# Memory attention at the start of layer 1, pair steps dealt out by table, six state updates moved into the output projection, and an own PSUM bank for the first query and the first forget gate

## The chip, the cores and the metric

The kernel is one launch on one core of a Trainium2 chip. The metric is device time in microseconds (us): 906.13 us is the median of three runs of the kernel before (906.07 to 907.13). Engines are named as in the profile: PE is the matrix engine (PEld its weight loads), DVE, ACT and POOL are the vector, scalar and general engines, SP issues most loads. L303 is line 303 of the kernel whose profile is read; lines of the changed kernel are a few higher.

## The reference, cut to what matters

One inference step of a decoder with two layers, for 256 prompt tokens and 8 sample tokens (264 columns) of width 2048. Layer 0 mixes tokens by windowed attention, layer 1 by a gated recurrence (HGRN2) with 12 heads, whose state is 128x128 for each head and sample. In both, 4 more heads attend to a memory of 256 rows, a SiLU gate multiplies all 2048 channels, and one output projection, a residual and a LayerNorm follow.

```python
def _hgrn2_chunked(q, k, v, logf, s0):
...
    state = jnp.exp(g_last)[..., None] * state + jnp.einsum('bshk,bshv->bhkv', k_dec, vc)
...
def _hgrn_branch(h, w_in, lb, norm_w, s0):
    q, f, iv, mq, g = _split(jnp.einsum('btd,de->bte', h, w_in), HG_SPLITS)
    fg = lb[None, None, :] + (1.0 - lb[None, None, :]) * jax.nn.sigmoid(f.astype(jnp.float32))
    qh = jax.nn.silu(q.astype(jnp.float32)).reshape(b, t, HG_HEADS, HG_DK)
    kh = (1.0 - fg).reshape(b, t, HG_HEADS, HG_DK)
...
    o, s_new = _hgrn2_chunked(qh, kh, vh, gh, s0.astype(jnp.float32))
    o = o * lax.rsqrt(jnp.mean(jnp.square(o), axis=-1, keepdims=True) + RMS_EPS) \
        * norm_w.astype(jnp.float32).reshape(HG_HEADS, HG_DV)
...
def _mem_attend(mq, mk, mv):
    s = jnp.einsum('bthd,bmhd->bhtm', mq, mk).astype(jnp.float32) * (MEM_HD ** -0.5)
    p = jax.nn.softmax(s, axis=-1)
    return jnp.einsum('bhtm,bmhd->bthd', p.astype(mv.dtype), mv)
```

## The kernel before, in words

**The stream of units.** The kernel is a stream of 172 units, most of them a block of 128x2048 fp32 (1 MB): a weight's 2048 input rows by 128 output columns, a block of a memory cache, or a state. SP loads a unit into one of four `raw` buffers (L76 to L82). `prep` (L84) splits it into a high and a low fp16 half in one of four `hl` buffers: ACT writes the high half (L97), DVE the low half (L98). Four `hl` buffers mean that unit n+4 is split only when PE has done with unit n. A weight unit is then 48 matmuls of 128x264 (three for each of 16 blocks, L303, L304, L305), accumulated in one PSUM bank. The eight last units of the output projection are split into buffers of their own (`held`).

**PSUM.** Eight banks with fixed tags: two `pj` for projections, two `pt` for small transposes and products, two `sc` for scores, one `pv`, one `ms`. A tag with two buffers is handed out in turn, in program order: whoever asks third waits for the first to be read.

**Layer 1 before.** For each of six pairs of heads come the units f, f, v, v, q, state, q, state: forget gates (`f_unit`), values (`hv_unit`), queries (`hq_unit`) and the two heads' states in half units of 512 KB (`state_unit`). For heads 0 to 7 a gate unit stands behind each state. Then come four memory query units (mq), eight memory cache units (ck, cv) between gate units 8 to 15, and 16 units of the output projection (o). `hv_unit` reads its bank at L1034 (`hvt`) and L249/L251 (`vs`, the sample tokens' values); one unit later `hv_rows` transposes them on PE (`hvp`, L1045, and `hvr`, L1048) and copies them out. The tile `vs` is one buffer for each head parity: it can't be written before `hvr` of the pair before has read it, and the `pj` bank is free only when `vs` is written.

**The side chain of a pair.** `hg_side` (L1064) computes the prompt part of the recurrence for two heads. It is a generator; after each unit, `pump(1)` issues one step of it. Its steps are hd, seven levels hs, pk, pu, hpo (L1117 to L1171), and rms (L1182), with `osb` (L1173), `osq` (L1177), a Ln and an Exp on ACT (L1183, L1186, each with a table load), and the scaled result on DVE (L1189). It takes `sc`, `pt` and `pv` banks between the units' own uses.

**State update before.** Inside each `state_unit`, after its eight products for the sample outputs (`hos`), eight matmuls with a selection matrix spread the values (`vb`, L1233), ACT scales the state by the forget gate (L1237, 8 instructions per head), DVE adds key times value (L1238, 8 per head), and POOL stores the new state (`out_ss`, L1241).

**What sets the order.** Every engine works through its own list in order, and that list is fixed when the kernel is built: a scheduler takes the program's order as priority and places each instruction where, by its own durations, it is ready. What waits in a list holds up all that is behind it in that list.

## Time and profile before

| | before |
|---|---|
| median of three runs | 906.13 us |
| profiled execution: time, span, mean clock | 906.08 us, 904.3 us, 0.994 |
| PE busy | 886.6 us (98%) |
| DVE, ACT busy | 701.5 us (78%), 582.4 us (64%) |
| bytes moved | 198.67 MB, 220 GB/s |

The span goes from the first instruction to the last; the execution's own time is 1.8 us longer. PE's busy time counts from a matmul's start to its modelled end, so that matmuls which follow each other without a gap overlap in it; a gap appears as "idle before", with the instruction that ended the wait. PEclk is the clock that PE was granted, as a share of full speed.

### The profile page before, as it was taken

To read this page: it belongs to the slowest core of one execution; us is meant where nothing else is said; L and a number is where in the kernel's file an instruction comes from. 1 tells how busy PE (TensorE), PEld (TensorE's weight loads), DVE (VectorE), ACT (ScalarE), POOL (GpSimd) and SP (SyncE) were. 2 spreads that over 40 slices of the span, in tenths; PEclk is the share of its full clock that TensorE was granted. 3 is DMA by queue.
4 is the path that set the end of the run, shared out by engine and by line. 5 is a ranking of instruction groups with operands and counts; after the bars stand their busy time and mean duration, and the time that the engine had idled before them with its cause. 6 is when DMAs were issued, how large, how long until landed. Compare 5 with 4: busy or idle time off the path is not lost.

```text
span 904.3 us, 21814 instructions
## 1 busy us (share of the span) xinstructions
PE 886.6 (98%) x9281; PEld 762.9 (84%) x9281; DVE 701.5 (78%) x1230; ACT 582.4 (64%) x982; POOL 34.9 (4%) x68
## 2 busy tenths in 40 slices
PE   9999999999999999999999999999999999799996
PEld 6888889678888888876888888898888888688996
DVE  6879877669886666697687887979788989678736
ACT  6767776657664444476766877777777585858415
POOL 1100010000000000002000000000000000000000
PEclk9999999999999999999999999999999999899999
DMA  9998566557785555556374655827454878456303
GB/s 340 392 353 317 188 245 209 188 208 265 262 333 192 187 192 203 207 198 214 127 292 137 216 201 174 299 101 260 160 215 164 303 283 308 172 207 244 130 2 97
DMA packets 37853, 198.67 MB, mean 220 GB/s; under 512 B 4555, under 2 KB 10732, under 8 KB 17532
## 3 DMA queue, kind: packets, MB, share of 16 engines
q1 hardware_dynamic: 33024, 181.55, 56.3%
q0 software_dynamic: 4688, 15.67, 4.6%
q8 instruction: 72, 1.18, 0.5%
q14 instruction: 25, 0.20, 0.1%
q10 hardware_dynamic: 44, 0.07, 0.0%
HBM read 180.03 MB, written 17.22 MB: 218 GB/s over the span
## 4 chain that ended last, share of the span: by engine, by line
PE 77%; DVE 8%; ACT 6%; DMA 6%; issue 3%; SPq 0%; ACTq 0%; DVEq 0%
PE o L303 5%; PE o L305 5%; PE o L304 5%; PE g L305 5%; PE g L303 5%; PE g L304 5%; DVE hl L98 4%; ACT hl L97 2%; PE hv L305 2%; PE hv L303 2%; PE hv L304 2%; DMA raw<-in_w_in 2%; PE hq L303 2%; PE hq L305 2%; PE hq L304 2%
## 5 line engine op out<-in xcount | busy, mean ns | idle before, releaser
L98 DVE SCALAR_TENSOR_TENSOR hl<-raw,hl 128x2048 f16<-128x2048 f32 (+2 forms) x168 | 358.6, 2138 | 82.0 <-ACT hl L97 81.0
L97 ACT ACTIVATE hl<-raw 128x2048 f16<-128x2048 f32 (+2 forms) x168 | 299.2, 1784 | 97.8 <-PE o L305 45.4
L305 PEld LDWEIGHTS <-hl 128*128 128x128 f16 (+2 forms) x2048 | 197.4, 98 | 31.8 <-DVE hl L98 2.9
L303 PEld LDWEIGHTS <-hl 128*128 128x128 f16 (+2 forms) x2048 | 197.3, 98 | 30.6 <-issue 2.2
L304 PEld LDWEIGHTS <-hl 128*128 128x128 f16 (+2 forms) x2048 | 197.4, 98 | 30.3 <-issue 2.2
L305 PE MATMUL g<-xhl,hl 128*128 128x264 f16 x512 | 142.0, 277 | 2.4 <-DVE hl L98 2.4
L303 PE MATMUL g<-xhl,hl 128*128 128x264 f16 x512 | 141.9, 277 | 0.0
L304 PE MATMUL g<-xhl,hl 128*128 128x264 f16 x512 | 141.9, 277 | 0.0
L303 PE MATMUL o<-mix,hl 128*128 128x264 f16 x384 | 105.4, 276 | 0.8 <-DVE xres L747 0.8
L304 PE MATMUL o<-mix,hl 128*128 128x264 f16 x384 | 105.8, 276 | 0.0
L305 PE MATMUL o<-mix,hl 128*128 128x264 f16 x384 | 105.7, 276 | 0.0
L303 PE MATMUL q<-xhl,hl 128*128 128x264 f16 x192 | 53.0, 276 | 1.0 <-DVE kst L251 1.0
L303 PE MATMUL f<-xhl,hl 128*128 128x264 f16 x192 | 52.9, 276 | 0.4 <-DVE mvhl L251 0.4
L305 PE MATMUL hv<-xhl,hl 128*128 128x264 f16 x192 | 53.0, 276 | 0.0
L303 PE MATMUL hq<-xhl,hl 128*128 128x264 f16 x192 | 53.0, 276 | 0.0
L304 PE MATMUL hq<-xhl,hl 128*128 128x264 f16 x192 | 53.0, 276 | 0.0
L305 PE MATMUL hq<-xhl,hl 128*128 128x264 f16 x192 | 53.0, 276 | 0.0
L304 PE MATMUL hv<-xhl,hl 128*128 128x264 f16 x192 | 53.0, 276 | 0.0
L303 PE MATMUL hv<-xhl,hl 128*128 128x264 f16 x192 | 53.0, 276 | 0.0
L304 PE MATMUL q<-xhl,hl 128*128 128x264 f16 x192 | 53.0, 276 | 0.0
L305 PE MATMUL q<-xhl,hl 128*128 128x264 f16 x192 | 53.0, 276 | 0.0
L304 PE MATMUL f<-xhl,hl 128*128 128x264 f16 x192 | 52.9, 276 | 0.0
(338 smaller groups left out, 1858.4 us busy)
## 6 DMA issues: line engine op xcount, KB each, us to landing
raw<-in_w_in SPq DMA_DIRECT2D x88, 1024.0 KB, 6.4
raw<-in_w_o SPq DMA_DIRECT2D x32, 1024.0 KB, 5.0
raw<-in_w_mk SPq DMA_DIRECT2D x8, 1024.0 KB, 4.9
raw<-in_w_mv SPq DMA_DIRECT2D x8, 1024.0 KB, 4.9
raw<-in_c_mk SPq DMA_DIRECT2D x8, 1024.0 KB, 5.1
raw<-in_c_mv SPq DMA_DIRECT2D x8, 1024.0 KB, 7.0
raw<-in_state SPq DMA_DIRECT2D x12, 512.0 KB, 5.4
out_ss<-raw POOLq DMA_DIRECT2D x12, 512.0 KB, 5.5
```

Source lines behind the costliest of these rows:

```text
L97: hi = self.nc.scalar.activation(hl[:, 0, s], raw[:, s], AF.Copy, scale=scale)
L98: lo = self.nc.vector.scalar_tensor_tensor(hl[:, 1, s], raw[:, s], scale, hl[:, 0, s], op0=ALU.mult, op1=ALU.subtract)
L303: mm(out, lhs(0), rhs(0), start=start, stop=False)
L304: mm(out, lhs(0), rhs(1), start=False, stop=False)
L305: return mm(out, lhs(1), rhs(0), start=False, stop=stop)
```

## The change

The changed kernel computes the same; one scale moves from the keys into the selection matrix. It does this:

- **Own bank, high halves first.** q0 (the first projection of layer 0's queries) and f0 (the first unit of layer 1) accumulate in the `pv` bank instead of a `pj` bank, with all 32 products of the weight's high half first and the 16 of its low half last.
- **Memory attention first.** Layer 1 begins with f0, the four mq units and then the eight cache units, dealt between f1, v0, v1, q0, two gates, q1, f2 and f3. The four memory side chains (`memp_side`) run there too.
- **Pair steps by table.** `pump` takes the number of steps from a table: 0 after cache and state units, 2 after most f and v units, 1 otherwise. Before it was 1 after every unit.
- **States by pair.** One unit holds the states of two heads (1 MB). Heads 0 to 5 are updated there, one head at once and one a unit later; the `raw` buffer is held one unit longer.
- **Six updates put off.** For heads 6 to 11 the state unit only copies the forget gates and keys behind the spread values (`vr`) and stores that to DRAM (`kept`, 80 KB for a pair). POOL loads it back into `late_kept`, and loads each state a second time into the memory attention's old tiles `mkhl`, `mvhl`, `mqhl` ("homes"). The update runs as `late_update`, attached to output units 1, 3, 5, 7, 9 and 11; the loads of heads 9, 10 and 11 need a home whose store has landed.
- **Gates.** Only heads 0, 1, 2 and 6 have their gate early; all others, those of heads 10 and 11 last, stand between the pairs and the output units.

Three places show what the scheduler makes of it. In names the number behind the word is the head or the pair (hvr6: head 6; hpo2: pair 2 of heads 4 and 5), behind the underscore stands a buffer.

First, PE in layer 1 around the values and queries of heads 6 to 9. Before:

```order
L303 MATMUL hv7_8148<-xhl_93,hl113_7897 128x264
...
L303 MATMUL hq6_8231<-xhl_93,hl114_7992 128x264
...
L1152 MATMUL pk2_8214<-ident_66,qk32_4_7165 128x128 x4
L1045 MATMUL hvp6_8221<-ident_66,hvt6_8110 128x128 x2
...
L1048 MATMUL hvr6_8225<-ident16_68,vs0_5659 128x128
L1158 MATMUL pu2_8283<-vn4_7321,kn2_8219 128x128 x4
```

After:

```order
L1166 MATMUL pu2_8658<-vn4_7926,kn2_8599 128x128 x4
L1053 MATMUL hvp6_8681<-ident_66,hvt6_8545 128x128 x2
...
L309 MATMUL hv9_9267<-xhl_96,hl127_8979 128x264
L1179 MATMUL hpo2_8669<-qk32_4_7736,s12_8663 128x128
...
L1056 MATMUL hvr6_8685<-ident16_68,vs0_5662 128x128
L1053 MATMUL hvp7_8755<-ident_66,hvt6_8545 128x128 x2
...
L1056 MATMUL hvr7_8759<-ident16_68,vs1_5663 128x128
...
L307 MATMUL hq8_9343<-xhl_96,hl128_9076 128x264
```

The transposes of head 6's values (hvp6, hvr6), which stood inside the query unit of the same head, now stand one pair of heads later, at and behind the end of hv9, and directly ahead of the query unit of head 8.

Second, ACT at the same two places, where the values are read from their bank. Before (heads 6 and 7):

```order
L1034 ACTIVATE hvt6_8110<-hv6_8059 128x264
L249 ACTIVATE vs0_5659<-hv6_8059 128x8
L97 ACTIVATE hl116_8145<-raw116_7840 128x2048
L1079 ACTIVATE qk16_1_5654<-qk32_4_7165 128x2x8x32
L1079 ACTIVATE qk16_2_5655<-qk32_4_7165 128x2x4x64
L1034 ACTIVATE hvt6_8110<-hv7_8148 128x264
L249 ACTIVATE vs1_5660<-hv7_8148 128x8
```

After (heads 8 and 9; hl127 is hv9's unit, so that hl131 takes its buffer):

```order
L100 ACTIVATE hl131_9338<-raw131_8982 128x2048
L1181 ACTIVATE osb2_8187<-hpo2_8669 128x2x256
L1009 ACTIVATE qk32_8_9034<-th8_9036,hl_lb_88 128x256
L1009 ACTIVATE qk32_8_9034<-th9_9130,hl_lb_88 128x256
L1054 ACTIVATE vn6_8543<-hvp7_8755 128x256
L1042 ACTIVATE hvt8_9226<-hv8_9175 128x264
L253 ACTIVATE vs0_5662<-hv8_9175 128x8
L1042 ACTIVATE hvt8_9226<-hv9_9267 128x264
L253 ACTIVATE vs1_5663<-hv9_9267 128x8
L1185 ACTIVATE osq20_8677<-osb2_8187 128x264
L1185 ACTIVATE osq21_8679<-osb2_8187 128x264
L1213 ACTIVATE mkhl_100<-mkhl_100,late_kept_10622 128x128 x5
```

The readers of head 8's value bank (hvt8, vs0) now stand behind a split of a whole unit and the tail of pair 2, and a put-off state's scaling follows at once.

Third, DVE where pair 5 ends and its two mixes are made for the output projection. Before:

```order
L1164 SCALAR_TENSOR_TENSOR s25_10571<-s15_10570,prod5_10089,pu5_10565 128x128 x2
L671 TENSOR_SCALAR mrnm1_10691<-mrnm1_10691 32x1
L673 RECIPROCAL mrz1_10692<-mrz1_10692 32x1
L674 TENSOR_SCALAR mrows1_10690<-mrows1_10690,mrz1_10692 32x256
L251 SCALAR_TENSOR_TENSOR msphl1_10701<-mback1_10698,msphl1_10701 128x64
L1189 SCALAR_TENSOR_TENSOR mix_95<-osb5_9734,small_t_64,osq50_10644 128x264
```

After:

```order
L1172 SCALAR_TENSOR_TENSOR s25_10690<-s15_10689,prod5_10066,pu5_10684 128x128 x2
L1214 SCALAR_TENSOR_TENSOR mkhl_100<-vb60_11142,late_kept_10622,mkhl_100 128x128 x4
L1214 SCALAR_TENSOR_TENSOR mkhl_100<-vb61_11155,late_kept_10622,mkhl_100 128x128 x4
...
L1214 SCALAR_TENSOR_TENSOR mqhl_99<-vb80_11438,late_kept_10622,mqhl_99 128x128 x4
L1197 SCALAR_TENSOR_TENSOR mix_98<-osb5_10087,small_t_64,osq50_10763 128x264
L1197 SCALAR_TENSOR_TENSOR mix_98<-osb5_10087,small_t_64,osq51_10765 128x264
L1214 SCALAR_TENSOR_TENSOR mqhl_99<-vb81_11451,late_kept_10622,mqhl_99 128x128 x4
L737 SCALAR_TENSOR_TENSOR sil110_10951<-sil110_10951,mix_98 128x264
L737 SCALAR_TENSOR_TENSOR sil111_11011<-sil111_11011,mix_98 128x264
L739 TENSOR_TENSOR mix_98<-sil110_10951,mix_98 128x264
```

Where the memory softmax of the sample tokens stood, there are now 24 additions of the put-off updates of heads 6, 7 and 8 (three tiles, eight each), and the two mixes of pair 5 stand among them. Before, PE met this end of pair 5 inside gate unit 13; after, it meets it inside output units 10 and 11, whose last matmuls read these mixes.

The diff, cut to what the prediction speaks of:

```diff
-NG1 = 8
+EARLY = (0, 1, 2, 6)
+LATER = tuple(range(6, HD))
...
-            while free < prepped and (free <= i or self.units[free][5]):
+            while free < prepped and (free + self.longer.get(free, 0) <= i or self.units[free][5]):
...
-    def proj(hl, src, n, name, cols=slice(None), tag="pj"):
+    def proj(hl, src, n, name, cols=slice(None), tag="pj", apart=False):
         w = hl.rearrange("p s (c f) -> p s c f", c=NC)
+        if apart:
+            pt = bank("pv", 1, name)
+            for k, (c, s, r) in enumerate([(c, 0, r) for c in range(NC) for r in range(2)] + [(c, 1, 0) for c in range(NC)]):
+                mm(pt[:, :n], w[:, s, c], src[:, r, c, cols], start=k == 0, stop=k == 3 * NC - 1)
+            return pt[:, :n]
...
-            pt = proj(hl, xhl, T, f"f{h}")
+            pt = proj(hl, xhl, T, f"f{h}", apart=h == 0)
...
-                cur["vr"] = p1.tile([P, 2, P], F16, tag="vr", name=f"vr{h}", bufs=2)
+                cur["vr"] = p1.tile([P, 2, KEPT], F32, tag="vr", name=f"vr{h}", bufs=2)
...
+    def update(h, R, vr, fgs, ks, sel):
+        for g in range(2):
+            pvb = bank("pt", 2, f"vb{h}{g}")
+            for bb in range(4):
+                mm(pvb[:, bb * P : (bb + 1) * P], sel[:, 4 * g + bb], vr, start=True, stop=True)
+            for bb in range(4):
+                b = 4 * g + bb
+                s = R[:, b]
+                nc.scalar.activation(s, s, AF.Copy, scale=fgs[:, b : b + 1])
+                nc.vector.scalar_tensor_tensor(
+                    s, pvb[:, bb * P : (bb + 1) * P], ks[:, b : b + 1], s, op0=ALU.mult, op1=ALU.add
+                )
+        nc.gpsimd.dma_start(ss_o[h // 2, :, h % 2 * TS * P : (h % 2 + 1) * TS * P], R.rearrange("p b v -> p (b v)"))
+
+    homes = deque()
+    aside = {}
+
+    def fetch(h):
+        if not homes:
+            aside["sel"] = cp.tile([P, TS, P], F16, tag="ms", name="late_sel", bufs=2)
+            nc.gpsimd.dma_start(aside["sel"], sel_d)
+            aside["kept"] = cp.tile([P, len(LATER), KEPT], F32, tag="ms", name="late_kept", bufs=2)
+            for pi in sorted(kept):
+                k = 2 * pi - LATER[0]
+                nc.gpsimd.dma_start(aside["kept"][:, k : k + 2], kept[pi])
+            for t in (mkhl, mvhl, mqhl):
+                names = "abcd"[: len(t.shape) - 1]
+                homes.append(t.bitcast(F32).rearrange(f"p {' '.join(names)} -> p ({' '.join(names)})")[:, : TS * P])
+        homes.rotate(-1)
+        aside[h] = homes[-1]
+        nc.gpsimd.dma_start(aside[h], state[h // 2][:, (h % 2) * TS * P : (h % 2 + 1) * TS * P])
+
+    def late_update(h):
+        k = aside["kept"][:, h - LATER[0]]
+        R = aside[h].rearrange("p (b v) -> p b v", b=TS)
+        update(h, R, k[:, : P // 2].bitcast(F16), k[:, P // 2 : P // 2 + TS], k[:, P // 2 + TS :], aside["sel"])
+
+    def with_update(fn, k):
+        def f(hl):
+            fn(hl)
+            late_update(LATER[k])
+            if k + 3 < len(LATER):
+                fetch(LATER[k + 3])
+
+        return f
+
...
+            if 2 * pi in LATER:
+                tail = vr[:, :, P // 2 :]
+                nc.vector.tensor_copy(tail[:, :, :TS], fgs)
+                nc.vector.tensor_copy(tail[:, :, TS:], ks)
+                nc.gpsimd.dma_start(kept[pi], vr)
+                return
+            R = raw.rearrange("p (i b v) -> p i b v", i=2, b=TS)
+
+            def half(i):
+                update(2 * pi + i, R[:, i], vr[:, i, : P // 2].bitcast(F16), fgs[:, i], ks[:, i], H["sel"])
+
+            half(0)
+            later.append(lambda: half(1))
 
         return fn
 
...
+    state_at, pumps = {}, {}
+
+    def w1(part, i, fn, n=1):
+        pumps[len(stream.units)] = n
+        stream.add(wb(w_in1, NB1[part] + i), fn)
+
+    def state_of(pi):
+        at = state_at[pi] = len(stream.units)
+        pumps[at] = 0
+        whole = 2 * pi not in LATER
+        if whole:
+            stream.longer[at] = 1
+        stream.add(state[pi], state_unit(pi), SA, whole=whole)
+
...
+    f_of(0)
+    for h in range(NM):
+        w1("mq", h, mem1_sides(mq_unit(h)) if h == NM - 1 else mq_unit(h))
+    cache(c_mk, ck_unit, 0)
+    f_of(1, 2)
+    cache(c_mk, ck_unit, 1)
+    v_of(0, 2)
+    cache(c_mk, ck_unit, 2)
+    v_of(1)
+    cache(c_mk, ck_unit, 3)
+    q_of(0)
+    gate_of(0)
+    cache(c_mv, cv_unit, 0)
+    gate_of(1)
+    cache(c_mv, cv_unit, 1)
+    q_of(1)
+    cache(c_mv, cv_unit, 2)
+    f_of(2, 2)
+    cache(c_mv, cv_unit, 3)
+    f_of(3, 2)
+    state_of(0)
+    v_of(2, 2)
+    v_of(3, 2)
+    q_of(2)
+    q_of(3)
+    state_of(1)
+    gate_of(2)
+    for pi in range(2, HD // 2):
+        gated = 2 * pi - 2 in EARLY
+        f_of(2 * pi, 2)
+        f_of(2 * pi + 1, 2)
+        v_of(2 * pi, 2)
+        v_of(2 * pi + 1, 1 if gated else 2)
+        q_of(2 * pi)
+        q_of(2 * pi + 1)
+        state_of(pi)
+        if 2 * pi in EARLY:
+            gate_of(2 * pi)
...
+    for k, j in enumerate([j for j in range(NC) if j not in EARLY and j not in last] + list(last)):
+        w1("g", j, fetch_first(gate_unit(1, j)) if k == 6 else gate_unit(1, j))
     for i in range(NC):
-        stream.add(wb(w_o[1], i), out_unit(1, i), home=hold if i >= NC - NSPLIT else None)
+        unit = out_unit(1, i)
+        if i % 2 == 1 and i // 2 < len(LATER):
+            unit = with_update(unit, i // 2)
...
-        pump(1)
+        pump(pumps.get(i, 1))
...
```

## The prediction

> **What bounds the kernel now.** I read the page, then the windows of stages, the waits of PE, and the timeline of PE in the stretch with the waits. The page first:

> ```profile
> span 904.3 us, 21814 instructions
> PE 886.6 (98%) x9281; PEld 762.9 (84%) x9281; DVE 701.5 (78%) x1230; ACT 582.4 (64%) x982; POOL 34.9 (4%) x68
> ```

> PE bounds it. An edit counts only where it changes PE's work or PE's idle time. Windows of layer 1 (span, PE, PEld, DVE, ACT, POOL busy; then granted clock, DMA share, GB/s):

> ```profile
> 420.00:762.00 342.00, 341.60 (x3685) 302.55 (x3685) 285.65 (x530) 246.93 (x419) 14.69 (x27) 1.00 0.61 216
> 762.00:790.00 28.00, 22.50 (x280) 18.23 (x278) 20.70 (x31) 21.19 (x32) 0.54 (x1) 0.88 0.54 195
> ```

> In 342 us of pair work PE stands still for 0.4 us. In the next 28 us, where pair 5's end, the memory softmax and the last gates meet, it stands still for 5.5 us at a clock of 0.88. PE's waits inside 762 to 790, then two of the whole run:

> ```profile
> PE g L305 <- DVE hl L98: 2.4, 2, 1.7
> PE hpo L1169 <- ACT st L1147: 1.5, 1, 1.5
> PE mback L677 <- DVE mrows L674: 1.0, 1, 1.0
> PE msc L303 <- ACT osq L1183: 0.4, 1, 0.4
> PE hpo L1171 <- ACT s L1162: 0.3, 1, 0.3
> ```

> ```profile
> PE q L303 <- DVE kst L251: 1.0, 1, 1.0
> PE f L303 <- DVE mvhl L251: 0.4, 1, 0.4
> ```

> The timeline around the longest of these gaps (start, us), and the windows of two throttled stretches (columns as above):

> ```profile
> 783.32 0.27 PE L303 MATMUL g<-xhl,hl 128*128 128x264 f16 x1
> 783.43 0.27 PE L304 MATMUL g<-xhl,hl 128*128 128x264 f16 x1
> 785.43 0.40 PE L305 MATMUL g<-xhl,hl 128*128 128x264 f16 x1 [1.73 <-DVE hl L98]
> 785.63 0.43 PE L303 MATMUL g<-xhl,hl 128*128 128x264 f16 x1
> 785.85 0.43 PE L304 MATMUL g<-xhl,hl 128*128 128x264 f16 x1
> ```

> ```profile
> 777.00:781.00 4.00, 3.63 (x54) 2.85 (x53) 0.67 (x2) 3.96 (x7) 0.00 (x0) 0.64 0.27 107
> 785.40:788.10 2.70, 2.67 (x13) 1.84 (x14) 2.70 (x5) 2.70 (x6) 0.00 (x0) 0.50 0.50 161
> ```

> A weight's matmul starts 0.11 us after the one before (48 make 5.4 us for a unit); after the gap of 1.73 us they start 0.22 us apart for 2.7 us. So this stretch loses 5.5 us of idle time, 1.4 us (0.36 of 4.0) and 1.35 us (half of 2.7) by the clock, and 0.17 us in each of its six gaps, since a gap is counted from the modelled end (0.28 after the start) where the next matmul could have come 0.11 after it: 9.3 us in all.

> **The change, part by part.** *Own bank, high halves first.* q0 waits for the bank that kst is read from, f0 for that of mvhl, the one 1.0 and the other 0.4 us, with 0.17 each: 1.7 us. In the `pv` bank both waits go; the low halves come 32 matmuls (3.6 us) later than before, so nothing is late next. −1.7 us.

> *Memory attention first.* The softmax and the cache units leave the stretch 762 to 790 and stand beside the first pairs, where no side chain of a pair is behind yet. I count the whole −9.3 us there, and judge what comes back by the ends of the pairs, next.

> *The pairs.* Two steps a unit put pk and pu ahead of hvp in the turn of the two `pt` banks, and pair p's chain now ends while pair p+1's values are projected (first place of the change). The query unit that follows needs the `pj` bank that `vs` is read from; `vs` needs `hvr` of the pair before, and ACT's readers stand behind a unit's split and the chain's tail. The durations, from ACT's timeline in 600 to 640, 545 to 600, and 762 to 790:

> ```profile
> 607.87 0.58 ACT L1173 ACTIVATE osb<-hpo 128x512 f32<-128x512 f32 x1
> 608.35 1.90 ACT L97 ACTIVATE hl<-raw 128x2048 f16<-128x2048 f32 x1
> 610.15 0.73 ACT L1177 ACTIVATE osq<-osb 128x264 f32<-128x264 f32 x2
> 613.74 1.28 ACT L1183 ACT_TABLE_LOAD   x1
> 615.04 0.85 ACT L1183 ACTIVATE osq<-rms,eps_rms 128x264 f32<-128x264 f32 x2
> 634.55 0.59 ACT L1001 ACTIVATE qk<-th,hl_lb 128x256 f32<-128x256 f32 x1
> ```

> ```profile
> 587.04 2.44 ACT L1237 ACTIVATE raw<-raw,fg 128x128 f32<-128x128 f32 x8
> 589.89 0.38 ACT L1034 ACTIVATE hvt<-hv 128x264 f32<-128x264 f32 x1
> 590.16 0.17 ACT L249 ACTIVATE vs<-hv 128x8 f16<-128x8 f32 x1
> ```

> ```profile
> 771.06 0.36 ACT L1147 ACTIVATE st<-hs 64x256 f32<-64x256 f32 x1
> 771.32 0.58 ACT L1154 ACTIVATE kn<-pk 128x512 f32<-128x512 f32 x1
> 773.15 0.38 ACT L1162 ACTIVATE s<-pu 128x256 f32<-128x256 f32 x1 [1.25 <-PE pu L1158]
> ```

> From one start to the next a split takes 1.80, osb 0.48, hvt 0.27: each 0.1 less than its row. On PE and DVE:

> ```profile
> 772.02 1.09 PE L1158 MATMUL pu<-vn,kn 128*128 128x128 f32 x8
> 774.13 0.39 PE L1170 MATMUL hpo<-st,vn 128*128 128x128 f32 x2
> 774.35 0.39 PE L1171 MATMUL hpo<-qk,s 128*128 128x128 f32 x2
> 776.01 1.16 PE L1182 MATMUL rms<-osq,ones_rms 128*128 128x264 f32 x4
> ```

> ```profile
> 567.61 1.90 DVE L1238 SCALAR_TENSOR_TENSOR raw<-vb,ks,raw 128x128 f32<-128x128 f32 x7
> 570.43 2.29 DVE L98 SCALAR_TENSOR_TENSOR hl<-raw,hl 128x2048 f16<-128x2048 f32 x1
> ```

> All times below count from the end of the pair's second value unit; 0.2 us is my estimate for a hand-over between engines.

> - *hq6 (A).* The same list as in the second place of the change, for head 6, and here both rms stand ahead of hq6. ACT: split 1.80, osb 0.48, two qk 0.98, vn and hvt 0.54, vs 0.06, hvt and vs 0.33, osq 0.4, so 4.6, and 4.8 on PE. Then two rms (1.0) and a vb: hq6 starts at 6.0. PE has 2.8 us of its own there (four hpo at 0.22, two rms, some 0.9 of small ones). Stall 3.2.
> - *hq8 (B).* Up to vs 4.0, on DVE behind the split's low half (1.9 + 2.2): hq8 starts at 4.5, with 1.2 of PE's own. Stall 3.3.
> - *hq10 (C).* Here PE has even pk, hpo and pu behind hv11. Split 1.8, st and kn 0.85, pu 0.93, s 0.4, four hpo 0.9, osb, qk, vn, hvt, vs 2.2, and hand-overs 0.6: hq10 starts at 7.7, with 3.5 of PE's own. Stall 4.2.

> *The put-off updates beside them.* For pairs 3 and 4, ACT's scalings of `mkhl` and `mqhl` stand ahead of the Ln that frees the `sc` bank for hd3 and hd4. They wait for `late_kept`: a store and a load in turn on POOL's queue, 80 KB each. Such transfers aren't in the trace; the nearest rows are

> ```profile
> ident<-in_ident POOLq DMA_DIRECT2D x1, 64.0 KB, 3.8
> out_sp<-s POOLq DMA_DIRECT2D x6, 128.0 KB, 3.1
> raw<-in_state SPq DMA_DIRECT2D x12, 512.0 KB, 5.4
> out_ss<-raw POOLq DMA_DIRECT2D x12, 512.0 KB, 5.5
> ```

> I take 3.8, the nearest in size, with 3.1 and 5.5 as ends. B: the values are copied at 2.3, loaded back at 9.9; five scalings at 0.30, a table load 1.3 and a Ln 0.5 make 13.2; PE comes to hd3 at 11.3 (hq8, two rms, part of hq9). Stall 1.9 (0.5 to 5.3). C: copied at 6.3, back at 13.9, eight scalings, table, Ln: 18.1; PE is there at 14.1. Stall 4.0 (2.6 to 7.4). [...]

> *Output units 10 and 11 (D).* Times from the end of pu5. DVE's adds take 0.26 each. The first can start at 2.4, when PE has done the 19 matmuls of o11 ahead of vb60; five groups of four are done at 7.85. ACT's chain from hpo at 3.3 (osb, osq, rms, table, two Ln 0.85, table, Exp) brings the mixes' factors at 8.6; the two mixes take 0.9 (264 columns each, an estimate from osq's row, as for Exp and the gate products), four more adds 1.0, two gate products and ACT's product after them 1.0: o10 goes on at 11.5. PE's own: 2.1, hpo 0.9, rms 1.0, eight groups vb 1.8, so 5.8. Stall 5.7. Then vb101 and o12 need head 9's state, whose load waits for head 6's store in the same tile: issued at 4.7, 5.5 and 5.4 later it is there at 15.7; eight scalings, one add and one residual add end at 18.9. PE comes there at 15.9 (36 matmuls). Stall 3.0. D is 8.7.

> *Work that changes without weight.* The second read of six states (3 MB), the kept tiles and the larger state loads go beside DMA engines that are busy 61% in the pairs; twelve ones products less save PE 0.3 us at most; DVE saves some small splits while it isn't the bound. Nothing, as long as weights arrive a unit ahead; if that cover went, a late unit would cost up to its 5.4 us.

> *Clock.* A gap of 1.73 us cost 1.35 more; the gaps of 1.0 (q0) and 0.4 (f0) cost none that I see. Six of the stalls are 1.9 us or longer; D's first is in pieces. Between 0 and 6 x 1.35 = 8.1, I take 4.0, the middle. [...]

> **The sum**, against the profiled execution's 906.1 (span 904.3 and 1.8 around it; the median of the runs is 906.13, the same): −1.7 −9.3 +3.2 +(3.3+1.9) +(4.2+4.0) +8.7 +4.0 = +18.3, so 924.4.

> **The rivals.** *Nothing comes in place (faster).* If the readers of the value banks were through ACT's list, and the kept tiles back, before PE asks at hq6, hq8, hq10 and o10, only −11.0 would be left: 895. For it: 342 us of the same work with 0.4 us idle, ACT at 64%. Against it: PE's list shows the small steps of a pair's end in one heap ahead of hq6, hq8 and hq10, where nothing else is left to cover them, as it was at 769 to 778. It decides where ACT's lists run 3 to 4 us shorter than added up here.

> *Only the lists, not the loads.* If DMAs land early enough and the clock holds, A, B, C and the first of D stay: 3.2 + 3.3 + 4.2 + 5.7 = 16.4, and 906.1 − 11.0 + 16.4 = 911.5. For it: POOL's queue is nearly empty there, and the two mixes don't need the loads.

> *The clock bites at every stall, and transfers are slow.* 8.1 in place of 4.0, and 3.4 more each for B and C: 935.

> *The first bank edit does nothing.* `pv` has one buffer; if its last reader is late, q0 and f0 wait as before: +1.7 on any case.

> **How the numbers follow.** A measurement here can tell about 0.2%, 1.8 us. Chances: my sum, 914 to 930, 0.55; lists only, 903 to 914, 0.18; clock and slow transfers, above 930, 0.12; nothing in place, below 903, 0.15. The range 901 to 932 leaves out most of the last and of the third. Faster by over 0.2% is the last case and a little of the second, 0.16; within 0.2% a slice of the second, 0.03; slower 0.81. The predicted time is 924.

> **What would show it.** In the changed profile: no wait of q0 on kst, of f0 on mvhl, and no `mback` among PE's waits late in layer 1; gaps of 3 to 4 us ahead of hq6 (or its rms) and hq8, hq10, with vs or osq as what ended them; hd on Ln, with a scaling (L1213) ahead of that on ACT; 5 to 6 us inside o10 and o11, ended by mix, and some 3 us ahead of o12 that end with the load of `mkhl`. I am wrong if PE goes through hv7 to hq6 without a gap, or if waits of weight units on splits (hl) fill the pairs.

## The result, and the profile after

| | before | after |
|---|---|---|
| median (four runs each, same chip) | 906.57 us | 928.16 us |
| lowest, highest | 906.07, 907.13 | 926.54, 928.39 |
| ratio, 95% interval | | 1.0237 (1.0224 to 1.025) |
| profiled execution: time, span, mean clock | 906.08, 904.3, 0.994 | 928.13, 926.4, 0.990 |

The changed kernel is 21.6 us slower. Its page first:

```profile
span 926.4 us, 21727 instructions
PE 893.8 (96%) x9269; PEld 764.9 (83%) x9269; DVE 694.9 (75%) x1176; ACT 580.6 (63%) x964; POOL 42.0 (5%) x81
```

PE has nearly the same work (9269 matmul records against 9281), so the span grew by waiting and, as shown further down, by a lower clock. Windows of the changed kernel, the first two being the stretches shown of before (span, then PE, PEld, DVE, ACT, POOL busy; clock, DMA share, GB/s):

```profile
420.00:762.00 342.00, 327.94 (x3521) 285.69 (x3519) 262.32 (x419) 234.30 (x381) 14.71 (x27) 0.99 0.60 214
762.00:790.00 28.00, 28.00 (x276) 24.80 (x275) 20.42 (x38) 18.24 (x27) 1.62 (x3) 1.00 0.47 162
790.00:870.00 80.00, 73.08 (x697) 63.10 (x696) 65.45 (x108) 52.16 (x72) 4.82 (x9) 0.98 0.63 226
```

The 5.5 us that PE stood still between 762 and 790 are gone, as forecast. In their place PE stands still for 14.1 us in the pairs, where it was 0.4, and for 6.9 us in the output units (790 to 870). Output units carry the layer in front of their number, as in the kernel's names: output units 10, 11, 12 and 16 are the first, second, third and seventh of layer 1's sixteen, while the list of put-off updates in the change counts 1, 3, 5 and so on without it. PE's waits after (total, times, longest):

```profile
PE hq L307 <- DVE vs L255: 4.8, 2, 2.9
PE hs L307 <- ACT qk L1087: 3.4, 4, 1.2
PE vb L1209 <- DVE mqhl L1214: 2.8, 2, 2.1
PE o L307 <- DVE xres L756: 2.7, 3, 1.8
PE vb L1209 <- ACT vn L1054: 1.6, 1, 1.6
...
PE hpo L1177 <- ACT st L1155: 1.2, 1, 1.2
PE hd L1128 <- ACT osq L1191: 1.1, 2, 0.7
PE rms L1190 <- ACT osq L1185: 1.1, 2, 0.6
PE vb L1209 <- DVE mvhl L1214: 0.9, 1, 0.9
PE lnq L814 <- ACT xhl L768: 0.8, 1, 0.8
PE o L307 <- ACT mix L738: 0.4, 1, 0.4
PE vb L1209 <- DVE vr L1057: 0.3, 1, 0.3
PE hpo L1179 <- ACT s L1170: 0.3, 1, 0.3
```

No row has q0 on kst, f0 on mvhl, or mback. The two on `vs` are hq8 and hq10; `vb` on `vn` and `vr` is head 4's update ahead of hq6. PE's timeline around hq8 shows the transposes of the values directly ahead of it, and the matmuls behind it at half pace (0.22 us apart):

```profile
661.64 0.39 PE L1053 MATMUL hvp<-ident,hvt 128*128 128x128 f32 x2
662.12 0.22 PE L1056 MATMUL hvr<-ident,vs 128*128 128x128 f16 x1
665.28 0.38 PE L307 MATMUL hq<-xhl,hl 128*128 128x264 f16 x1 [2.94 <-DVE vs L255]
665.46 0.43 PE L308 MATMUL hq<-xhl,hl 128*128 128x264 f16 x1
665.68 0.43 PE L309 MATMUL hq<-xhl,hl 128*128 128x264 f16 x1
```

### The profile page after: what moved, and what is told of

It is laid out like the page before. It is cut to its first block, busy times and chain, and to the rows that moved or that the text cites. A ratio compares the mean times of both kernels' runs of the same rounds, so it can differ in the third digit from the quotient of the medians.

```text
span 926.4 us, 21727 instructions
## 1 busy us (share of the span) xinstructions
PE 893.8 (96%) x9269; PEld 764.9 (83%) x9269; DVE 694.9 (75%) x1176; ACT 580.6 (63%) x964; POOL 42.0 (5%) x81
## 4 chain that ended last, share of the span: by engine, by line
PE 64%; issue 25%; ACT 4%; DVE 3%; DMA 2%; POOL 1%; ACTq 0%; POOLq 0%; DVEq 0%
PE g L307 6%; PE g L308 6%; PE g L309 6%; PE o L307 4%; PE o L308 4%; PE o L309 4%; PE q L309 2%; PE q L308 2%; PE q L307 2%; PE mk L307 2%; PE mk L309 2%; PE mk L308 2%; PE mv L600 1%; PE mv L602 1%; PE mv L601 1%
## 5 line engine op out<-in xcount | busy, mean ns | idle before, releaser
L308 PEld LDWEIGHTS <-hl 128*128 128x128 f16 (+2 forms) x2016 | 194.9, 98 | 36.3 <-issue 8.0
L307 PEld LDWEIGHTS <-hl 128*128 128x128 f16 (+2 forms) x2016 | 194.9, 98 | 30.9 <-issue 2.2
L309 PEld LDWEIGHTS <-hl 128*128 128x128 f16 (+2 forms) x2016 | 194.8, 98 | 28.8 <-issue 0.2
L307 PE MATMUL hq<-xhl,hl 128*128 128x264 f16 x192 | 54.5, 284 | 4.9 <-DVE vs L255 4.8
L309 PE MATMUL hq<-xhl,hl 128*128 128x264 f16 x192 | 54.3, 283 | 0.0
L308 PE MATMUL hq<-xhl,hl 128*128 128x264 f16 x192 | 54.2, 282 | 0.0
L307 PE MATMUL q<-xhl,hl 128*128 128x264 f16 x176 | 48.6, 276 | 0.0
L308 PE MATMUL q<-xhl,hl 128*128 128x264 f16 x176 | 48.6, 276 | 0.0
L309 PE MATMUL q<-xhl,hl 128*128 128x264 f16 x176 | 48.6, 276 | 0.0
L309 PE MATMUL f<-xhl,hl 128*128 128x264 f16 x176 | 48.6, 276 | 0.0
L308 PE MATMUL f<-xhl,hl 128*128 128x264 f16 x176 | 48.6, 276 | 0.0
```

Of the source, the lines that this page charges most:

```text
L307: mm(out, lhs(0), rhs(0), start=start, stop=False)
L308: mm(out, lhs(0), rhs(1), start=False, stop=False)
L309: return mm(out, lhs(1), rhs(0), start=False, stop=stop)
```

## The experiments

Before the first runs I had three theories. **Theory 1**, the prediction's: the table of steps brings pk, pu and hpo of one pair together with hvp and hvr of the next, in the `pt` banks and in ACT's list. **Theory 2**: the put-off updates cost it. **Theory 3**: memory attention ahead of the pairs costs it by itself. Times below are medians beside runs of before on the same chip (906.0 to 906.7); ratios have 95% intervals.

**The first edit alone** (in the kernel before).

```diff
...
-            pt = proj(hl, xhl, T, f"q{j}")
+            pt = proj(hl, xhl, T, f"q{j}", apart=j == 0)
...
-            pt = proj(hl, xhl, T, f"f{h}")
+            pt = proj(hl, xhl, T, f"f{h}", apart=h == 0)
```

> The kernel before with only the first edit: q0 and f0 in the pv bank, high halves first. The sum's own term (each wait and 0.17 us with it): 1.7 us faster than before, about 904.9, and neither wait of PE is left. Rival (pv's last reader is late, or the low halves come no earlier than the bank): within 0.5 us of before. [...]

905.39 us, ratio 0.9989 (0.9977 to 1.0002). Two of PE's four longest waits in this kernel:

```profile
PE mpo L303 <- ACT mphl L249: 1.7, 1, 1.7
...
PE msc L303 <- ACT ms L619: 1.1, 1, 1.1
```

The waits of q0 and f0 are gone. But the memory softmax, late in layer 1, makes PE wait in two places here where the profile of before has no such row, and by the ratio 1.0 us is left of the 1.7; the interval takes in no gain at all.

**One step a unit.**

```diff
-        pump(pumps.get(i, 1))
+        pump(1)
```

> The changed kernel with one step of a pair's chain after every unit, in place of the table of 0, 1 and 2. Theory 1 (the table brings the end of a pair's chain, with its pk and pu, into the two pt banks and the lists just where the next pair's values need hvp, hvr and the tiles hvt and vs): the stalls ahead of hq6, hq8 and hq10 go, 4.8 + 4.7 + 6.3 us with their clock, most of the 2.6 and 3.1 behind them goes too or moves to another place, so 908 to 916 against 928.2; the stall in output units 10 and 11 stays or grows by up to 4 us, since pair 5's chain now ends there. Theory 2 (the put-off updates are what costs): 925 to 929, hq8 and hq10 still wait. Theory 3 (memory attention ahead of the pairs by itself): 925 to 929.

918.62 us, 1.012 (1.0095 to 1.0144). The waits of hq on `vs` are gone, but 918.6 lies above the forecast: in 790 to 870 PE is busy for 70.18 us, where it was 73.08, and the clock is 0.91, where it was 0.98.

```profile
790.00:870.00 80.00, 70.18 (x674) 60.51 (x673) 65.32 (x117) 46.84 (x68) 5.33 (x10) 0.91 0.53 193
```

**More value tiles.**

```diff
-                cur["vt"] = p1.tile([P, 2, T], F32, tag="vt", name=f"hvt{h}", bufs=1)
+                cur["vt"] = p1.tile([P, 2, T], F32, tag="vt", name=f"hvt{h}", bufs=2)
...
-        H["vs"] = [p1.tile([P, P], F16, name=f"vs{i}") for i in range(2)]
+        H["vs"] = [p1.tile([P, P], F16, name=f"vs{i}") for i in range(4)]
...
-            vs = H["vs"][i]
+            vs = H["vs"][h % 4]
```

> The changed kernel, table and all, with two buffers for hvt in place of one and four vs tiles in place of two (s1 and s2 get one buffer each to make room). Theory 1 in its narrow form (what closes the circle is the reuse of hvt and vs: a value unit can't be read from its bank before hvr of the pair before): the waits of hq8 and hq10 on vs go, and the heaps ahead of hq6, hq8 and hq10 with them, 4.8 + 4.7 + 6.3 us: 912 to 917 against 928.2, with D in output units 10 to 16 as it was. If only the turn of the pt banks and ACT's list count, less than 5 us comes back (923 to 927). Theories 2 and 3: 926 to 929.

920.12 us, 1.0149 (1.0122 to 1.0176). Again no wait on `vs`, again above the forecast, and the loss moved to the same place, where PE is busy for 67.13 of 80 us at a clock of 0.94. The rows of this kernel's first and last `hd` and `rms` (duration min/median/max, first and last start) show something else:

```profile
L1128 PE MATMUL hd<-hqs,qk x48: 272/275/276, 488.5 to 785.9; 128*128 128x128 f32 x48
L1190 PE MATMUL rms<-osq,ones_rms x24: 386/386/491, 556.4 to 813.3; 128*128 128x264 f32 x24
```

The last chain begins at 785.9, among the last gates, and ends at 813.3, in the output units. A fault in the place where chain and values meet doesn't do that; a chain that is late would.

**None put off.**

```diff
-LATER = tuple(range(6, HD))
+LATER = ()
```

> The changed kernel with all twelve states updated in their state units (none put off; no kept tile, no second load). Theory 1: the heaps ahead of hq6 and hq10 stay (4.8 and 6.3 us, hq8 perhaps smaller), the two waits behind kept transfers (2.6 and 3.1) and the stalls in output units 10 to 18 (7.3 and about 3) go: 911 to 916 against 928.2. Theory 2: everything that came is due to them: 895 to 900. If the adds and scalings, back in the pairs, fill ACT and DVE there, new waits of the value units eat the gain: 918 to 926.

923.36 us, 1.0184 (1.0162 to 1.0206): the last of the three cases. Theory 2 falls, since 16.7 of the 21.6 us remain. The scalings, back in the pairs, stand in a row ahead of a split and, at 708.90, a level's `qk` on ACT, and PE waits 5.4 us for that `qk`:

```profile
702.41 4.78 ACT L1213 ACTIVATE raw<-raw,fg 128x128 f32<-128x128 f32 x16 [1.17 <-DVE hl L101]
707.10 1.89 ACT L100 ACTIVATE hl<-raw 128x2048 f16<-128x2048 f32 x1
```

And output units 10 and 11 stall without any update there, behind the last rms:

```profile
822.11 1.16 PE L1190 MATMUL rms<-osq,ones_rms 128*128 128x264 f32 x4 [1.14 <-ACT osq L1185]
828.05 0.60 PE L307 MATMUL o<-mix,hl 128*128 128x264 f16 x2 [4.78 <-ACT mix L738]
```

**Theory 4**, formed here. The `side` queue steps one chain at a time: a chain's hd comes when the chain before is through. The first and last `hd` and `rms` of before, then of the changed kernel:

```profile
L1120 PE MATMUL hd<-hqs,qk x48: 272/275/275, 459.3 to 731.3; 128*128 128x128 f32 x48
L1182 PE MATMUL rms<-osq,ones_rms x24: 386/386/490, 506.9 to 776.8; 128*128 128x264 f32 x24
```

```profile
L1128 PE MATMUL hd<-hqs,qk x48: 272/275/377, 489.5 to 774.5; 128*128 128x128 f32 x48
L1190 PE MATMUL rms<-osq,ones_rms x24: 386/386/809, 557.5 to 819.6; 128*128 128x264 f32 x24
```

From the first rms to the last are five chains: 54.0 us each before, 52.4 after. The pace is nearly the same, but not for the same reason: before, ten steps at one for each unit of 5.4 us also make 54, so there it may be the units' own pace, while after it is PE that waits. Before, the first four pairs brought ten units each, the last two eight, and twenty units stood behind the pairs. Now memory attention stands ahead, twelve gates stand behind, and a pair from the third on brings six weight units of 5.4 us and a state (the fourth one gate more). The units outrun the chain. The transposes of a pair's values stand behind pk and pu of the chain (the order that the prediction read), so `hvt` and `vs` are not yet read and stop the next pair's values: that is the heap at hq6, hq8 and hq10. And since memory attention and its four chains come first, the first hd is 30 us later; the first chain, from its first hd to its first rms, takes 68 us in place of 48; and the last rms is 43 us later, in output unit 11, where nothing is left for PE to do beside it, since every output unit needs the last mixes. The stalls in the pairs and D would be one lag.

**A shorter chain** (two of the seven levels are left out, so it computes something else; `SLOT` and `f`, not shown, only keep the tiles in step).

```diff
...
-        for now, ahead in (((1, 2), (4, 8)), ((4, 8), (16, 32)), ((16, 32), (64,))):
+        for now, ahead in (((1, 2), (4, 8)), ((4, 8), (64,))):
```

> The changed kernel with a shorter side chain: the levels 16 and 32 of the recurrence are left out (2 of the 10 steps of each pair, with their products, splits and masks; what is computed is not the recurrence any more). Theory 4, formed from the three runs before: the six chains run one after another, each 45 to 50 us from hd to rms and the next hd 5 us later, and the units of a pair (38 us) outrun them until hvt and vs stop the values; the stalls at hq6, hq8, hq10 and in output units 10 and 11 are all this one lag. Then with 8 steps the lag is gone, the heaps dissolve, the last rms stands among the gates: 928.2 - 5 (PE work left out) - 15.8 - 5.7 - about 8 = 892 to 901. Theory 1 (two steps a unit bring pk, pu and hpo together with hvp and hvr): they still meet, and most of the 15.8 stays: 908 to 922.

894.92 us, 0.987 (0.9842 to 0.9898), as theory 4 has it. This kernel's last rms stands 60 us earlier, from one chain's rms to the next are 42.0 us ((759.9 − 550.0) / 5), and PE hardly waits in the pairs. Since PE is busy there throughout, 42.0 may again be the units' pace, and the chain's own can be shorter:

```profile
L1193 PE MATMUL rms<-osq,ones_rms x24: 386/386/469, 550.0 to 759.9; 128*128 128x264 f32 x24
```

```profile
600.00:750.00 150.00, 149.37 (x1564) 131.84 (x1562) 119.45 (x187) 106.37 (x173) 5.41 (x10) 1.00 0.59 208
790.00:870.00 80.00, 77.78 (x898) 71.98 (x896) 58.52 (x111) 37.86 (x58) 4.80 (x9) 1.00 0.48 182
```

The table, the put-off updates, memory attention first and the single `hvt` all stand as in the changed kernel. The levels also take 19 us of DVE, 8 of ACT and 144 matmuls with them, so this run doesn't part the chain's length from the load on the engines.

**Kept in SBUF.**

```diff
...
-                cur["vr"] = p1.tile([P, 2, KEPT], F32, tag="vr", name=f"vr{h}", bufs=2)
+                    cur["vr"] = aside["kept"][:, h - LATER[0] : h - LATER[0] + 2]
...
-                nc.gpsimd.dma_start(kept[pi], vr)
...
-                nc.gpsimd.dma_start(aside["kept"][:, k : k + 2], kept[pi])
```

> The changed kernel with the spread values, forget gates and keys of heads 6 to 11 written straight into late_kept: no kept tile in DRAM, no store and load in turn. By my sum the waits at hd3 and hd4 go, 1.9 and 4.0 us with their share of the clock (2.6 and 3.1 measured, those of hs behind them included): 921 to 924 against 928.2. Theory 4: the chains of pairs 4 and 5 start 1 to 3 us earlier, all else as it was: 924 to 927.

922.55 us, 1.0175 (1.015 to 1.02): 5.6 us less than the changed kernel, the prediction's 5.9. The waits of hd and hs are gone, those at hq8 (2.9) and in output units 10 and 11 stay. Head 10's unit no longer waits on `vs` (1.9), but hpo and hvp wait there for 2.5.

**Eight gates early.**

```diff
-EARLY = (0, 1, 2, 6)
+EARLY = tuple(range(8))
...
+            gate_of(2 * pi + 1)
```

> The changed kernel with eight gates among the pairs, two behind each state of pairs 0 to 3, and eight behind the pairs in place of twelve. Theory 4: with 49 us of units a pair the values are outrun less: the waits at hq6, hq8 and hq10 (15.8 us with their clock) shrink to under 4 us, but only eight gates cover the last chain, which ends deeper in the output units: there 15 to 25 us in place of 10; in all 917 to 930, the same loss in another place. Theory 1: the heaps ahead of hq6, hq8 and hq10 stay, as the table still gives two steps to a unit: 928 or more, with the waits of hq on vs still in the list.

919.9 us, 1.0141 (1.0116 to 1.0166). No hq waits any more, although the table still gives two steps to a unit; what is left in the pairs is mainly hs on `qk` (between 420 and 762 PE stands still for 6.7 us in place of 14.1), and 790 to 870 is worse, 71.78 of 80 us busy at a clock of 0.94:

```profile
PE hs L307 <- ACT qk L1087: 6.5, 6, 3.0
```

This is theory 4 against theory 1: pk and pu of pair 2 still stand ahead of head 6's hvp (starts 653.3, 655.8 and 656.7, in the changed kernel 655.2, 658.6 and 659.5), yet more units a pair dissolve the heap, and fewer gates behind the pairs leave the last chain uncovered.

**Memory attention between pairs 3 to 5** (in the kernel of the first experiment, with a second queue for its chains; the rest of the edit is the order of the units, told below).

```diff
...
         pump(1)
+        pump_beside(sides.get(i, 0))
```

> The kernel before with q0 and f0 in the bank of their own, one step after every unit, half states and no update put off; gates 0 to 5 early; the four memory queries among pair 3, the key caches between the units of pair 4, the value caches between those of pair 5, with the four memory side chains stepped beside the pairs' own instead of in their turn; then ten gates. Theory 4: the first chain starts as early as before (about 458), every pair has 49 us of units or more, and ten gates stand behind the last chain, so neither the stretch 762 to 790 nor the output units stall: 895 to 899 against 906.6. If memory attention beside the pairs costs by itself (theory 3), or its softmax in the chains' banks: 903 to 912.

910.35 us, 1.0041 (1.0027 to 1.0054): a miss. The output units run (78.93 of 80 us), but among pairs 3 and 4 PE stands still for 7.9 us, where before had none:

```profile
600.00:750.00 150.00, 142.12 (x1651) 123.97 (x1650) 126.24 (x231) 112.52 (x187) 3.76 (x7) 0.99 0.63 225
```

Its rms go from 506.7 to 805.8, 59.8 us for a chain on average: 51 and 57 for the first two, 60 to 70 for the three with memory attention beside them. Here filler that brings its own splits and softmax goes with a slower chain, which it should cover.

**The chain's instructions ahead of the splits**, in the changed kernel and, with 600 and 200 places, in the kernel of the first experiment.

```diff
-                    next(side[0])
+                    with tc.high_priority(600) if side[0].gi_code.co_name == "hg_side" else nullcontext():
+                        next(side[0])
```

> The changed kernel, all of it, with each step of a pair's side chain given priority (600 places in the scheduler's order), so that its small ACT and DVE instructions stand ahead of the units' splits in the lists. Theory 4 (the chains, one after another at 48 to 56 us, are what PE waits for): the chains take less than 45 us each, the last rms stands before the end of the gates (before 805 against 819), the stalls in output units 10 and 11 go and those at hq6, hq8 and hq10 shrink: 898 to 912 against 928.2. If the chains' own length isn't set by what stands ahead of it in ACT's and DVE's lists, nothing moves (925 to 929). New waits of weight units on late splits would take back up to 5.

> The kernel before with the own bank for q0 and f0 and the same priority of 600 for the pair chains; nothing else of the change. Theory 4: the sixth chain ends some 20 us earlier, apart from the memory softmax and the last gates, so most of the 9.4 us of the stretch 762 to 790 goes: 896 to 901 against 906.6 (904.9 is the sum's value for the bank alone). If that stretch is bound by the memory softmax or by splits, not by the chain: 903 to 907.

> The same kernel with a priority of 200 places, so that a step moves ahead of fewer splits. Theory 4: the sixth chain ends some 5 to 10 us later than with 600 and meets the last gates, fewer splits come late: 897 to 903. Without an effect of the chain: 903 to 907.

939.93 us (1.0353, 1.0316 to 1.0389), 935.05 (1.0314, 1.0281 to 1.0347) and 936.38 (1.0321, 1.0291 to 1.0352): all three missed, by some 30 us. In the first of them the units wait in the chain's place, for an early gate's result (`mix`) that now stands behind it and a split in DVE's list, and the chain waits as well:

```profile
PE f L308 <- DVE mix L744: 3.8, 2, 2.0
PE hs L308 <- ACT qk L1088: 3.6, 7, 1.1
```

Its last rms is at 824.0. On theory 4 the times settle nothing; that a chain which takes its step out of turn also holds up the values that it needs is my reading, not shown. In part the chain did what theory 4 says: in the first of them the chains of pairs 2, 3 and 4 take 42, 40 and 44 us from first hd to last rms, where the changed kernel has 51, 46 and 48, but the first takes 104.

**The first pair ahead of memory attention** (in the changed kernel, memory chains beside; pairs 0 to 3 also go back to one step a unit).

```diff
-    f_of(0)
-    for h in range(NM):
-        w1("mq", h, mem1_sides(mq_unit(h)) if h == NM - 1 else mq_unit(h))
+    fill = {
+        1: [lambda h=h: mq_of(h) for h in range(NM)],
+        2: [lambda t=t: cache(c_mk, ck_unit, t) for t in range(4)],
+        3: [lambda t=t: cache(c_mv, cv_unit, t) for t in range(4)],
+    }
...
```

> The changed kernel with its memory attention taken from ahead of the first pair: the four memory queries stand between the units of pair 1, the key caches between those of pair 2, the value caches between those of pair 3, one step a unit there, and the memory side chains are stepped beside the pairs' own in place of ahead of them in one queue. Six updates stay put off, pairs 4 and 5 keep two steps a unit and 38 us of units. Theory 4 (one chain after another, 48 to 56 us each, the first begun 30 us later than before): the first hd comes at about 455 in place of 489, nothing stalls at hq6 (4.8), the last rms comes at 790 to 805 in place of 819, so the stall in output units 10 and 11 (7.3) shrinks to under 4; hq8 and hq10, where the units still outrun the chain, keep half or more of their 16.7: 906 to 916 against 928.2. If the place of memory attention doesn't matter: 925 to 929. If its softmax beside the pairs costs more than it spares, as in the run with memory between pairs 3 to 5: above 916.

917.4 us, 1.0122 (1.0105 to 1.014), just outside, in the case where the softmax beside the pairs costs more than it spares. The first hd comes at 453.5, nothing stalls at hq6, hq8 still waits 3.3 us and the output units less than in the changed kernel (76.21 of 80 us busy). But the last rms is at 810.9, not 790 to 805: from rms to rms it takes 91 and 67 us where memory attention stands beside, then 43, 49 and 49. Theory 3 is right in part: memory attention, taken from ahead of the first pair, gave back 10.8 us together with the single steps of the first pairs, which this run doesn't part.

## Why the prediction was right, and where it was off

The forecast was 924; 928.16 lies in its range. That it came so near owes something to luck: 3.0 us were forecast at output unit 12 and didn't come, and 3.0 us came later that no term had. Term by term, with 0.17 us added to each gap as in the prediction:

| term | forecast | measured |
|---|---|---|
| q0 and f0 | −1.7 | −1.7 |
| stretch 762 to 790 | −9.3 | −9.3 |
| A, hq6 | 3.2 | 3.0 (gaps 0.3, 1.6, 0.6) |
| B, hq8 | 3.3 | 3.1 |
| C, hq10 | 4.2 | 3.8 (gaps 1.2, 0.3, 1.9) |
| hd3, hd4 and what follows | 1.9 + 4.0 | 5.5 (hd 1.1, hs 3.4) |
| D, output units 10 and 11 | 5.7 | 5.4 (0.5, 0.9, 0.7, 2.1, 0.4) |
| output unit 12 | 3.0 | 0 |
| later waits on xres and xhl | 0 | 3.0 (2.7 and 0.8 in four gaps, less 0.8 in two of before) |
| clock | 4.0 | 6.2 |

These make 19.0 of the 22.1 us between the spans; the remaining 3.1 us are not accounted for. The 0.2 us that the sum took for a hand-over between engines was an estimate of mine that rests on no row; in before's trace s starts 0.04 us after pu's end (at 773.15), hpo 0.05 after s's end (773.58) and mback 0.15 after mrows' end (775.73). Point by point:

- *The lists at hq6, hq8, hq10.* Place, order and size were right. The reason was not whole. "Two steps a unit put pk and pu ahead of hvp" is how the lists read; with the same order and more units (eight gates early) there is no heap. It takes the order, which ties the values to the chain (with one step a unit head 6's hvp starts 42 us ahead of pair 2's pk, and nothing waits on `vs`), and a chain that can't keep up, and the prediction named no pace for it. So it also missed that the stalls in the pairs and D go together: one step a unit and more value tiles took the one away, and PE stood still 3 to 6 us longer at the other, at a lower clock.
- *The kept tiles.* The sum took 7.6 us for a store and a load in turn. The page after has medians:

```profile
kept<-vr POOLq DMA_DIRECT2D x3, 80.0 KB, 3.1
late_kept<-kept POOLq DMA_DIRECT2D x3, 80.0 KB, 2.2
```

  They make 5.3, but the transfers that ACT waited for were slower. For pair 3 it is 7.3 us from the store's issue to the scaling, much as forecast, 5.2 of it the load; for pair 4 it is 5.6 (713.61 to 719.17). Of the 5.5 us that came only 1.1 fell at hd: ACT stood 4.66 us for the load at 670.52, and what lay behind in its list, the Ln and then each level's `qk`, came late in turn:

```profile
663.18 0.54 POOL L1284 DMA_DIRECT2D kept<-vr  x1 [1.65 <-DVE prod L1097]
665.33 0.54 POOL L1229 DMA_DIRECT2D late_kept<-kept  x1 [1.61 <-DMA kept<-vr]
```

```profile
670.52 1.57 ACT L1213 ACTIVATE mkhl<-mkhl,late_kept 128x128 f32<-128x128 f32 x5 [4.66 <-DMA late_kept<-kept]
...
673.40 0.48 ACT L1191 ACTIVATE osq<-rms,eps_rms 128x264 f32<-128x264 f32 x1
```

- *Output unit 12* is the step that failed. "Stall 3.0" took head 9's state to land at 15.7 from pu5's end; it was scaled from 828.31 on, 14.1 us after pu5's end (814.2), and PE came to head 10's vb at 831.07, 16.9 after it in place of 15.9, without a wait. What the sum had too long is head 6's store in the same tile: 3.2 us (819.18 to the load's issue at 822.35) in place of 5.5. Later output unit 16 waited 1.79 us for a residual add that stood behind splits in DVE's list; that the late scalings and adds made these late is not shown, since ACT's splits from 849 on also waited for weights (0.9, 0.6 and 1.2 us):

```profile
828.31 2.44 ACT L1213 ACTIVATE mkhl<-mkhl,late_kept 128x128 f32<-128x128 f32 x8 [2.41 <-DMA mkhl<-in_state]
```

```profile
831.07 0.61 PE L1209 MATMUL vb<-late_kept,late_sel 128*128 128x128 f16 x8
...
855.43 0.27 PE L307 MATMUL o<-mix,hl 128*128 128x264 f16 x1 [1.79 <-DVE xres L756]
```

- *The clock* cost more than the middle taken. In the changed kernel PE runs at half pace in these four stretches, at A, B, C and D, and is busy for 12.4 us of them; at full pace that work would take half as long (at C a weight's matmuls start 0.22 us apart at a clock of 0.50, and 0.11 just ahead of it at 1.00), so by this estimate 6.2 us are lost:

```profile
613.47:616.88 3.41, 3.23 (x12) 2.36 (x13) 2.64 (x13) 3.25 (x6) 0.53 (x1) 0.50 0.74 252
664.67:668.08 3.41, 2.80 (x13) 1.92 (x13) 0.73 (x3) 1.18 (x6) 0.54 (x1) 0.50 0.51 163
715.87:719.28 3.41, 3.41 (x16) 2.40 (x14) 0.00 (x0) 0.11 (x1) 0.54 (x1) 0.50 0.13 34
825.10:828.50 3.40, 2.99 (x16) 1.91 (x14) 1.12 (x4) 0.96 (x3) 1.02 (x2) 0.50 0.89 283
```

- *The first rival* (nothing in place, 895) is near what the shorter chain gave, 894.9, but with work left out that was put at 5 us of PE's time ahead of that run: some gain is there if the chains keep up.

Open: what sets a chain's 52 us. With more value tiles the sixth took 27 us (785.9 to 813.3), with PE waiting on it, so it isn't the chain's own work alone; that it is the splits ahead of it in ACT's and DVE's lists is argued. The priority runs speak for it in three chains of one run and not in their times. No kernel here that computes the same beats before by more than the first edit's unclear 0.1%.

## What to carry to other kernels

Where a serial side chain runs beside a stream of units, work out its pace (first to last of one of its instructions, by the count), whether that pace is its own or the stream's, and how much stream each of its turns brings. Where the chain was the slower, taking filler out of the stream here gained nothing; it moved the waiting to where buffers run out and to the end. A heap of small instructions ahead of one unit can be a lag as much as a conflict on a bank: look for both. And before work is put ahead of such a chain, count how much later its last turn ends, and whether anything is left there to cover it.

## What the runs showed of the hardware

```profile
855.40:862.00 6.60, 6.57 (x60) 5.73 (x60) 6.60 (x10) 3.83 (x3) 0.00 (x0) 1.00 1.00 398
```

Each of the four half-paced stretches of *The clock* is 3.41 us long, and from start to start it is 51.2, 51.2 and 109.2 us, that is 15, 15 and 32 times 3.41. The two stretches of before, from 778.14 and 784.97, start 6.83 us apart, two times 3.41. After C's 1.86 us matmuls started 0.11 us apart, and 0.22 apart from 715.87 on, where the third stretch starts. In the 3.41 us ahead of each of the four stretches PE is busy for 1.01, 0.99, 1.46 and 0.67 us, and for 2.16 ahead of before's second. Yet 3.41 us of the changed kernel with 1.62 us busy, which end nine times 3.41 after the fourth stretch's start, were followed by full pace, so PE's busy time in them doesn't decide alone either, and what does stays open:

```profile
781.55:784.97 3.42, 2.16 (x78) 1.87 (x75) 3.42 (x6) 3.42 (x5) 0.00 (x0) 1.00 0.00 0
```

```profile
852.40:855.81 3.41, 1.62 (x18) 1.33 (x16) 3.41 (x5) 2.19 (x2) 0.00 (x0) 1.00 1.00 401
```
